# Score blocks of the prompt's attention on a third PSUM bank, the sample's results in the ring of the maxima, and a new pace for the sample beside the attention

## The chip, the cores and the metric

The kernel runs on one core of a Trainium2 chip. The metric is the device time of one execution in microseconds; lower is better. Three runs of the kernel before are shown below, and one further execution was profiled.

## What is computed

One inference step of a small decoder: one recurrent layer (RG-LRU), then one layer of forgetting attention, for a prompt of 2048 new tokens and for a *sample* of 8 sequences with 8 new tokens each, which look back on 4096 cached tokens in pages of 128 rows. There are 16 heads of 64. What the change touches is the attention, for the prompt and for the sample:

```python
def fox_block(q, k, v, cq, ck, q_pos, k_pos):
    s = jnp.einsum('bqhd,bkhd->bhqk', q, k).astype(jnp.float32) * (HEAD_DIM ** -0.5)
    s = s + jnp.swapaxes(cq, 1, 2)[:, :, :, None] - jnp.swapaxes(ck, 1, 2)[:, :, None, :]
    mask = k_pos[None, :] <= q_pos[:, None]
    s = jnp.where(mask[None, None], s, -jnp.inf)
    p = jax.nn.softmax(s, axis=-1)
    return jnp.einsum('bhqk,bkhd->bqhd', p.astype(v.dtype), v)
...
    past_k = cache_k[page_table].reshape(Bs, past_len, N_HEADS, HEAD_DIM)
    past_v = cache_v[page_table].reshape(Bs, past_len, N_HEADS, HEAD_DIM)
```

The prompt's attention is causal over 2048 positions. The sample reads every cached page, 16.8 MB of keys and values for each of 16 *turns* (a turn is one sequence and one half of the heads).

## The kernel before

The kernel's main line computes the recurrent layer, the projections, then the prompt's attention (`attention`, on the chip from about 1725 us to 2867 us), then the output projection (`project`). A second line of work, the sample (`decode`), is a Python generator that is advanced beside the main line: `Side.along(gen, share)` takes one step of the main generator, adds up the cost that it yields, and then advances the sample until the sample's own summed cost has reached `share` times that. This gives the order in which the program is written. From it a scheduler with a model of the engines' times lays down one fixed order for each engine: the earliest instruction in the program's order that is ready by the model goes first, so a later one may pass an earlier one that is not ready. On the chip each engine then goes through its list in that order and waits at semaphores. Two sample turns of the 16 (`FIRST`) lie beside an earlier stage, four and a half lie beside the projections, and the rest lies beside the attention.

**The prompt's attention.** A *unit* is one head and one of four groups of 512 queries; it has 4, 8, 12 or 16 *score blocks* of 128 keys by up to 512 queries, 640 blocks in all. For each block TensorE writes the transposed scores into a PSUM bank `st` with two matmuls (three on the diagonal, L1531, L1532, L1534), ScalarE takes the exponential into `p` (or `acc` for a unit's first block, L1540), and after each fourth block, two blocks later, `product` issues the matmuls with the values as one run (`ops`, L1551); then GpSimd adds each `p` to `acc` (L104), for the softmax's sums. The buffers: `st` has two banks, `p` has five (`NP`), `acc` five.

The maximum of each row is needed before its scores: `top` computes the scores a second time, coarsely, in the other orientation (`sx`, L1404), and VectorE reduces them (`mxs`, L1406, L1408). This runs some 8 to 18 blocks ahead of the scores. `sx` is a ring of three PSUM banks, which also takes the transposed maxima (`mps`), the sums (`tot`) and the broadcast reciprocals (`rp`).

**The sample.** A turn fetches 8 times 4 pages of keys and as many of values (`pages`, L1072, four 256 KB transfers each on SP's queue, into four buffers `raw`). VectorE transposes the keys (`ktr`, L1157); `scores` (L1125) multiplies with the queries, 64 matmul instructions in one run into a bank `dS`, which VectorE subtracts from the decay sums `sc`; `new_scores` (L1140) does it for the new rows. `softmax` uses small results `dm` (maxima) and `dsum` (sums); `products` (L1235) multiplies with the values into the bank `dO`, 16 instructions in one run; at the end `dres` (L1263) gathers the result. A run is made by `together`, which keeps its matmuls adjacent on TensorE.

**PSUM.** There are eight banks. The pool `psd` has two: tag "o" holds `dO` through a turn, tag "d" holds whichever of `dS`, `dm`, `dsum`, `dres` is in use, through `bank`. During the attention the pool `psa` has the other six: `ops` one, `st` two, `sx` three. After the sample has ended, the two banks of `psd` lie idle until the output projection. The sample's last step is followed by `project_ready`, which loads the weights of the output projection and splits them in eight steps.

The pace: `share = SHARE * (16 - FIRST) * TURN / (1024 / 128 * 24 * 4112 * 0.42 + 950000)` with `SHARE = 1.13` and `TURN = 22615`, one number for the projections and the attention. The attention yields `4.1 * (512 - lo) * 0.42` for each block and 213 for each tile of maxima.

Of the kernel before, what the change touches and what calls it, by code (L numbers as in the profile page):

```python
# [11 lines left out]
F32 = mybir.dt.float32  # L12
# [8 lines left out]
P = 128  # L21
# [6 lines left out]
H = 16  # L28
# [15 lines left out]
B_ORDER += [("g", c) for c in range(4)]  # L44

SHARE = 1.13
LEAD = 18
RAMP = 8
NS = 3
# [2 lines left out]
AHEAD = 8  # L52
FIRST = 2
NACC = 5
NP = 5
ADD = "G"
OG = 1
NQ = 6
# [14 lines left out]


SYNC = mybir.DependencyInfo(mybir.DependencyClass.Sync, mybir.DependencyReason.DATA)


def f(ap):
# [5 lines left out]
def tile_hawk_fox(  # L84
# [8 lines left out]
    V, A, G, T, S = nc.vector, nc.scalar, nc.gpsimd, nc.tensor, nc.sync  # L93
# [12 lines left out]
    def together(mms, after=()):  # L106

        first = mms[0]().ins
        for d in after:
            tc.add_manual_dep(first, d.ins.name, SYNC)  # L110
        with tc.high_priority(), tc.issue_after(first):
            for mm in mms[1:]:
                mm()


    xs_flat = x_sample.rearrange("b q d -> (b q) d")
# [94 lines left out]
    psum = {}  # L211
# [805 lines left out]
    TURN = 16 * QK + 33 * PV + 10 * HOP  # L1017


    known = set()  # L1020

    def decode(es, turns, nraw, nktr, ahead):
        pool = sbuf(es, "dec", "right")
# [25 lines left out]
        last, qbs = [], {}  # L1049

        def bank(name, tag="d"):
            return psum["dec"].tile([P, 512], F32, name=name, tag=tag, bufs=1)

        def spare():
# [52 lines left out]
        def keys(t, xs):  # L1107

            dl = t.dl
            b, hg, gmx = t.b, t.hg, t.gmx  # L1110

            def fetch_c():
                sc = t.sc = pool.tile([P, NPG // 4, 8, 32], F32, name="sc", tag="sc")
                S.dma_start(sc[:, :, :, :].rearrange("p x h i -> p (x h i)"),
                            c_d[hg, :, :, b].rearrange("m a x f -> (m a) (x f)").unsqueeze(1).to_broadcast([16, DS, 8 * 256]))
                t.cn = pool.tile([DS, 8, DS], F32, name="cn", tag="cn")
                S.dma_start(t.cn[:, :, :], cn_d[hg * 8:(hg + 1) * 8, b * DS:(b + 1) * DS].unsqueeze(0).to_broadcast([DS, 8, DS]))

            def scores(g, pp, kt):

                sp = bank("dS", "d" if ahead or pp == 0 else "o")

                def score(h, x, a):
                    blk = (h * 2 + x) * 32
                    return T.matmul(sp[a * 32:(a + 1) * 32, h * P:(h + 1) * P], qw[:, pp * 2 + h // 2, h % 2 * 2 + x, :],  # L1125
                                    kt[:, :, a, blk:blk + 32], start=(x == 0), stop=(x == 1))

                together([partial(score, h, x, a) for h in range(4) for x in range(2) for a in range(4)])
                sv = t.sc[:, g * 4:(g + 1) * 4, pp * 4:(pp + 1) * 4, :].rearrange("p n h i -> p h n i")
                tt(V, sv, sp[:, :].rearrange("p (h n i) -> p h n i", h=4, n=4), sv, ALU.subtract)  # L1130
                V.tensor_reduce(gmx[:, g, pp * 4:(pp + 1) * 4], sv, axis=AX.XY, op=ALU.max)

            def new_scores(raw):
                kx = (spare() if ahead else pool.tile([P, 512], F32, name="kx", tag="kx"))[:, :512]
                V.transpose(kx, raw[:, :])
                sp = bank("dS")

                def score(h, x):
                    blk = (h * 2 + x) * 32
                    return T.matmul(sp[:32, h * DS:(h + 1) * DS], qw[:, h // 2, h % 2 * 2 + x, :], kx[:, blk:blk + DS],  # L1140
                                    start=(x == 0), stop=(x == 1))

                together([partial(score, h, x) for h in range(8) for x in range(2)])
                tt(V, t.cn[:, :, :], sp[:DS, :64].rearrange("p (h j) -> p h j", h=8), t.cn[:, :, :], ALU.subtract)
                tt(V, t.cn[:, :, :], t.cn[:, :, :], maskN[:, :].unsqueeze(1).to_broadcast([DS, 8, DS]), ALU.add)
                V.tensor_reduce(gmx[:DS, 2, :], t.cn[:, :, :], axis=AX.X, op=ALU.max)

            for x in xs:
                g, n = divmod(x, 4)
                if n == 0:  # L1150
                    t.kts = [pool.tile([P, 4, 4, 256], F32, name="ktr", tag="ktr", bufs=nktr) for _ in range(2)]
                raw, _ = pages(cache_k, b, hg, x)
                if x == (3 if ahead else 0):
                    fetch_c()
                    t.rown = new_rows(ks_d, b, hg)
                for pp in range(2):
                    V.transpose(t.kts[pp][:, n], raw[:, :, pp * 256:(pp + 1) * 256])  # L1157
                    if n == 3:
                        dl.after(1 + pp, lambda g=g, pp=pp, kt=t.kts[pp]: scores(g, pp, kt))
                    if (g, n, pp) == (1, 0, 0):  # L1160
                        new_scores(t.rown)
                    dl.tick()
                    yield QK
# [59 lines left out]
        def values(t, xs):  # L1223

            dl = t.dl
            b, hg, sx, pc = t.b, t.hg, t.sx, t.pc
            if xs[0] == 0:
                t.op = bank("dO", "o")
            op = t.op

            def products(i, raw, came):

                def mm(d, a):
                    c = ((i + d) % 2 * 2 + a) * 32
                    return T.matmul(op[c:c + 32, :256], sx[:, d, i // 4, a * 4:(a + 1) * 4, :].rearrange("p h q -> p (h q)"),  # L1235
                                    raw[:, d, a * 256:(a + 1) * 256],
                                    start=(i + d < 2), stop=(i + d == NPG - 1))

                together([partial(mm, d, a) for d in range(4) for a in range(2)], came)

            def new_products(raw):
                for a in range(2):
                    T.matmul(op[a * 32:(a + 1) * 32, :256], pc[:, a * 32:(a + 1) * 32], raw[:, a * 256:(a + 1) * 256],
                             start=False, stop=True)

            for x in xs:
                raw, came = t.raws.pop(0) if t.raws else pages(cache_v, b, hg, x)
                dl.after(1, lambda i=x * 4, raw=raw, came=came: products(i, raw, came))
                if x == 5:
                    t.rown = new_rows(vs_d, b, hg)  # L1250
                yield 2 * PV
                dl.tick()
                yield 2 * PV
            if xs[-1] < 7:
                return
            dl.after(1, lambda: new_products(t.rown))
            dl.flush()
            ob = pool.tile([P, 256], F32, name="ob", tag="ob")
            A.copy(ob[:, :], op[:, :256])
            yield PV  # L1260
            sp = bank("dres")
            for pr in range(4):
                T.matmul(sp[:, pr * 16:(pr + 1) * 16], ob[:, pr % 2 * P:(pr % 2 + 1) * P], sel[:, pr * 16:(pr + 1) * 16],  # L1263
                         start=True, stop=True)
            for h2 in range(2):
                hp = slice(h2 * 64, (h2 + 1) * 64)
                pv_ = sp[hp, :64].rearrange("p (r h q) -> p r h q", r=4, h=2)
                rv = t.rb[hp, :].rearrange("p (r h q) -> p r h q", r=4, h=2)
                tt(V, oTs[hp, hg * 4:(hg + 1) * 4, b * DS:(b + 1) * DS], pv_[:, :, h2, :], rv[:, :, h2, :], ALU.mult)
# [37 lines left out]
    def attention(es):  # L1307
# [212 lines left out]
            yield 300  # L1520
        ops = acc = None
        pair = []
        for u, (h, qc) in enumerate(units):
            load_low(u + 2)
            for k in range(nks[u]):
# [1 line left out]
                qa, qb = qas[u], qbs[u % NQ]  # L1527
                lo = max(0, k - qc * 4) * P
                ks = slice(k * P, (k + 1) * P)
                ps = ps3.tile([P, 512], F32, name="st", tag="st", bufs=2)  # L1530
                T.matmul(ps[:, lo:], ka[:, ks], qa[:, lo:], start=True, stop=False)  # L1531
                T.matmul(ps[:, lo:], kb[:, ks], qb[:, lo:], start=False, stop=(k < qc * 4))  # L1532
                if k >= qc * 4:
                    T.matmul(ps[:, lo:lo + P], identB[:, :], causal[:, :], start=False, stop=True)  # L1534
# [38 lines left out]
                    load_head(h + 1)  # L1573
                yield 4.1 * (512 - lo) * 0.42 + (done[0] - before) * 213

    lent = {}

    rows = [(NSAMP, None, x1s_d[:, :], ys_flat)]
    rows += [(P, t, x1_d[t:t + P], yp_flat[t:t + P]) for t in range(SEQ - P, -1, -P)]
# [2 lines left out]
    def project_ready(es):  # L1582

        pool = sbuf(es, "projw", "right")
        proj["g"] = pool.tile([P, D], F32, name="bpostB")
        S.dma_start(proj["g"][:, :], b_post_norm.broadcast_to([P, D]))
        out = proj["out"] = Out(b_w_out[0], 0).place(pool)
        with ExitStack() as st:
            wpool["st"], wpool["ns"] = sbuf(st, "projs", "right"), 2
            out.fetch()  # L1590
            out.fetch()
            for i in range(8):
                yield 2000
                out.split(i + 1)
# [189 lines left out]
    def beside():  # L1784
        yield from decode(dec, turns[FIRST:], 4, 2, True)
        dec.close()
        yield from project_ready(last)

    side = Side(beside())
# [3 lines left out]
    wkeep.close()  # L1793
    lin.close()
    psum["att"] = banks(att, "psa", 6)
    side.along(attention(att), share)
    side.upto(1e12)
    project(last)
    att.close()
# [36 lines left out]
```

## Time and profile before

| | us |
|---|---|
| median of three runs | 3062.46 |
| the three runs | 3054.63, 3062.46, 3064.86 |
| the profiled execution's own time | 3055.27 |
| its span | 3053.6 |

The span is what the profile's rows cover; 1.7 us of the execution's own time lie around it. In the profile PE is TensorE, PEld its loading of weights, DVE VectorE, ACT ScalarE, POOL GpSimd, SP the engine whose queue issues nearly all transfers. L numbers are lines of the kernel. A row of waits reads "engine tile line <- what ended the wait: us in total, times, longest". TensorE's matmuls are pipelined, so that the rows of busy time overlap and a PE that is shown busy is not at its peak; the spacing of the starts is what tells its pace.

### The profile page before, as it was taken

How to read it: one execution, taken by the hardware profiler on the slowest of the kernel's cores; microseconds unless marked ns; L12 is line 12 of the kernel's file. 1: busy time of each engine (PE TensorE's matmuls, PEld its weight loads, DVE VectorE, ACT ScalarE, POOL GpSimd, SP SyncE). 2: the span in 40 equal slices, each digit the busy share in tenths (PEclk: the TensorE clock that was granted, in tenths of full speed). 3: DMA queues.
4: the chain of work that ended last, by engine and by line, in shares of the span. 5: the costliest groups of instructions: out<-in, count | busy, mean ns of one | idle time of the engine just before them, and what ended most of it. 6: DMA issues, size and time to landing. Idle time of an engine off the chain costs nothing.

```text
span 3053.6 us, 60463 instructions
## 1 busy us (share of the span) xinstructions
PE 2827.0 (93%) x21614; PEld 2258.5 (74%) x21614; DVE 1810.2 (59%) x4012; ACT 1269.8 (42%) x2874; POOL 1079.6 (35%) x1199
## 2 busy tenths in 40 slices
PE   6998999999999989998999799899899899999898
PEld 5997789988999978896888456565556565565687
DVE  7876465425357766765555566676767675554344
ACT  4665442222346655433333144343444345455311
POOL 1653201000016532000000366556465557587522
PEclk9999999999999999999999799899999999999999
DMA  4224546788622256999999988999999998323243
GB/s 122 81 85 133 175 125 203 240 268 263 216 83 89 83 185 194 316 320 320 330 311 315 294 274 268 299 275 308 306 298 319 322 297 258 92 65 86 84 145 111
DMA packets 492864, 653.41 MB, mean 214 GB/s; under 512 B 91099, under 2 KB 292828, under 8 KB 485285
## 3 DMA queue, kind: packets, MB, share of 16 engines
q1 hardware_dynamic: 488934, 643.87, 67.1%
q10 hardware_dynamic: 3340, 3.56, 0.5%
q8 instruction: 171, 2.80, 0.4%
q0 software_dynamic: 288, 2.10, 0.2%
q14 instruction: 131, 1.07, 0.1%
HBM read 513.82 MB, written 135.16 MB: 213 GB/s over the span
## 4 chain that ended last, share of the span: by engine, by line
PE 59%; DMA 18%; DVE 9%; ACT 5%; SPq 4%; issue 3%; POOL 2%; DVEq 0%; ACTq 0%; POOLq 0%
PE ops L1551 6%; PE y L368 4%; PE y L366 4%; PE y L367 4%; DMA raw<-in_cache_v_dram 4%; PE kv L366 4%; PE kv L367 4%; PE kv L368 4%; DMA raw<-in_cache_k_dram 4%; PE st L1531 3%; PE sx L1404 3%; PE dO L1235 3%; PE dS L1125 2%; PE st L1532 2%; PE qg L366 2%
## 5 line engine op out<-in xcount | busy, mean ns | idle before, releaser
L104 POOL TENSOR_TENSOR acc<-acc,p 128x512 f32<-128x512 f32 (+3 forms) x576 | 638.7, 1109 | 419.2 <-PE ops L1551 271.1
L1540 ACT ACTIVATE p<-st 128x512 f32<-128x512 f32 (+3 forms) x576 | 289.5, 524 | 404.9 <-PE st L1532 198.8
L1157 DVE STREAM_TRANSPOSE ktr<-raw 128x1024 f32<-128x1024 f32 x256 | 305.7, 1225 | 160.2 <-DMA raw<-in_cache_k_dram 157.8
L1406 DVE TENSOR_REDUCE mxs<-sx 128x1 f32<-128x512 f32 x384 | 253.1, 679 | 119.7 <-PE sx L1404 118.3
L367 PE MATMUL kv<-wl,xh 128*128 128x256 f32 (+3 forms) x1088 | 309.3, 287 | 11.2 <-DVE wl L411 11.0
L366 PE MATMUL kv<-wh,xh 128*128 128x256 f32 (+3 forms) x1088 | 310.8, 290 | 5.9 <-ACT wh L410 5.4
L368 PE MATMUL kv<-wh,xl 128*128 128x256 f32 (+3 forms) x1088 | 309.4, 287 | 0.0
L1531 PE MATMUL st<-qa,ka 128*128 128x512 f32 (+3 forms) x640 | 273.9, 428 | 12.2 <-ACT p L1540 11.0
L1551 PE MATMUL ops<-p,vvt 128*64 128x256 f32 (+1 forms) x2176 | 261.0, 366 | 3.4 <-ACT p L1540 2.8
L1404 PE MATMUL sx<-kbt,qbt 96*128 96x512 f32 (+3 forms) x640 | 236.9, 425 | 26.1 <-DMA qbt<-qd 12.0
L1532 PE MATMUL st<-qbt,kbt 128*128 128x512 f32 (+3 forms) x640 | 239.3, 374 | 0.0
L410 ACT ACTIVATE wh<-wst,gv 128x256 fp32r<-128x256 f32 (+1 forms) x384 | 164.5, 499 | 179.9 <-DMA wst<-in_b_w_in_dram 62.1
L411 DVE SCALAR_TENSOR_TENSOR wl<-wst,gv,wh 128x256 fp32r<-128x256 f32 (+1 forms) x384 | 170.5, 493 | 105.5 <-ACT wh L410 104.0
L1551 PEld LDWEIGHTS ops<-p,vvt 128*64 128x64 f32 x2176 | 161.2, 140 | 92.6 <-issue 22.7
L366 PE MATMUL qg<-xh,wh 128*128 128x384 f32 (+2 forms) x640 | 228.9, 359 | 0.0
L368 PE MATMUL qg<-xh,wl 128*128 128x384 f32 (+2 forms) x640 | 227.4, 356 | 0.0
L367 PE MATMUL qg<-xl,wh 128*128 128x512 f32 (+2 forms) x640 | 226.9, 356 | 0.0
L367 PEld LDWEIGHTS kv<-wl,xh 128*128 128x128 f32 (+1 forms) x1088 | 204.3, 189 | 14.9 <-DVE wl L411 12.6
L366 PEld LDWEIGHTS kv<-wh,xh 128*128 128x128 f32 (+1 forms) x1088 | 204.2, 189 | 12.0 <-ACT wh L410 6.4
L1090 POOL TENSOR_TENSOR qw<-qb,amask 128x128 f32<-128x128 f32 x64 | 29.3, 464 | 509.9 <-PE dS L1125 266.4
L368 PEld LDWEIGHTS kv<-wh,xl 128*128 128x128 f32 (+1 forms) x1088 | 205.6, 189 | 4.1 <-issue 4.1
L1531 PEld LDWEIGHTS st<-qa,ka 128*128 128x128 f32 x640 | 124.0, 194 | 109.9 <-issue 53.0
(297 smaller groups left out, 6370.0 us busy)
## 6 DMA issues: line engine op xcount, KB each, us to landing
raw<-in_cache_k_dram SPq DMA_DIRECT2D x512, 256.0 KB
raw<-in_cache_v_dram SPq DMA_DIRECT2D x512, 256.0 KB
wst<-in_w_kv_dram SPq DMA_DIRECT2D x48, 512.0 KB
wst<-in_b_w_in_dram SPq DMA_DIRECT2D x48, 512.0 KB
xt<-in_x_prompt_dram SPq DMA_DIRECT2D x32, 512.0 KB
wst<-in_a_w_in_dram SPq DMA_DIRECT2D x64, 256.0 KB
out_dram<-kf SPq DMA_DIRECT2D x128, 128.0 KB
sc<-cd SPq DMA_DIRECT2D x16, 1024.0 KB
```

What stands on the lines that cost most here:

```text
L104: eng.tensor_tensor(out, a, b, op=op)
L366: T.matmul(ps, lh(k), rh(k), start=(k == 0), stop=False)
L367: T.matmul(ps, lh(k), rl(k), start=False, stop=False)
L368: T.matmul(ps, ll(k), rh(k), start=False, stop=(k == nk - 1))
L411: V.scalar_tensor_tensor(wl[:, k, :], st[:, k, :], gk, f(wh[:, k, :]), op0=ALU.mult, op1=ALU.subtract)
L1157: V.transpose(t.kts[pp][:, n], raw[:, :, pp * 256:(pp + 1) * 256])
L1404: T.matmul(ps[:, :w], qb[0:96, j * P:(j + 1) * P], kb[0:96, ck * 512:ck * 512 + w], start=True, stop=True)
L1406: V.reduce_max(mx[:, j, ck:ck + 1], ps[:, :w], axis=AX.X)
L1531: T.matmul(ps[:, lo:], ka[:, ks], qa[:, lo:], start=True, stop=False)
L1532: T.matmul(ps[:, lo:], kb[:, ks], qb[:, lo:], start=False, stop=(k < qc * 4))
L1540: pair.append((k, lo, p, A.activation(p[:, lo:], ps[:, lo:], AF.Exp)))
L1551: return T.matmul(ops[r * HD:(r + 1) * HD, a0 * P:], vvs[h % 2][:, k, :], p[:, :].rearrange("p (a r c) -> p a r c", a=2, r=2)[:, a0:, r, : ...
```

## The change

Five edits:

1. `scores_bank` gives a score block its bank. As long as the sample runs, every third block takes tag "d" of `psd` and the others the two `st` banks. After the sample has ended (`dec_done`), every other block takes a bank of `psd`, "d" and "o" in turn, so that four banks go round.
2. In `decode`, once the attention's pool exists, `bank` gives what had tag "d" (`dS`, `dm`, `dsum`, `dres`) a bank of the ring `sx`, three banks shared with the maxima.
3. `together` returns its last matmul; `decode` notes it for each run of `scores` and `products`, and the first matmul of each score block gets an edge of order (no semaphore) to the last run that the program has written before it: on TensorE it is placed behind that run.
4. The sample's pace during the attention is worked out when the attention starts: what is left of the sample is spread over 88% (`SPAN`) of the attention's cost. The projections keep the former share.
5. `p` has six buffers in place of five.

```diff
+SPAN = 0.88
...
-NP = 5
+NP = 6
...
+ORDER = mybir.DependencyInfo(mybir.DependencyClass.NoSync, mybir.DependencyReason.DATA)
...
             for mm in mms[1:]:
-                mm()
+                last = mm().ins
+        return last
...
-    known = set()
+    known, run = set(), []
...
         def bank(name, tag="d"):
+            if tag == "d" and "att" in psum:
+                return psum["att"].tile([P, 512], F32, name=name, tag="sx", bufs=3)
             return psum["dec"].tile([P, 512], F32, name=name, tag=tag, bufs=1)
...
-                together([partial(score, h, x, a) for h in range(4) for x in range(2) for a in range(4)])
+                run.append(together([partial(score, h, x, a) for h in range(4) for x in range(2) for a in range(4)]))
...
-                together([partial(mm, d, a) for d in range(4) for a in range(2)], came)
+                run.append(together([partial(mm, d, a) for d in range(4) for a in range(2)], came))
...
+        wide = [0]
+
+        def scores_bank():
+
+            if dec_done:
+                wide[0] += 1
+                if wide[0] % 2:
+                    return psum["dec"].tile([P, 512], F32, name="st", tag="do"[wide[0] // 2 % 2], bufs=1)
+            else:
+                wide[0] += 1
+                if wide[0] % 3 == 0:
+                    return psum["dec"].tile([P, 512], F32, name="st", tag="d", bufs=1)
+            return ps3.tile([P, 512], F32, name="st", tag="st", bufs=2)
...
-                ps = ps3.tile([P, 512], F32, name="st", tag="st", bufs=2)
-                T.matmul(ps[:, lo:], ka[:, ks], qa[:, lo:], start=True, stop=False)
+                ps = scores_bank()
+                first = T.matmul(ps[:, lo:], ka[:, ks], qa[:, lo:], start=True, stop=False)
+                if run:
+                    tc.add_manual_dep(first.ins, run[-1].name, ORDER)
...
-    lent = {}
+    lent, dec_done = {}, []
...
         dec.close()
+        dec_done.append(True)
         yield from project_ready(last)
...
-    side.along(attention(att), share)
+    cost = sum(4.1 * 0.42 * (512 - max(0, k - qc * 4) * P) + 213 for qc in range(4) for k in range(4 * qc + 4)) * H
+    side.along(attention(att), ((16 - FIRST) * TURN - side.spent) / (cost * SPAN))
```

## The prediction

> **What bounds the kernel now.** I read the page first, then the busy time by stages, then the waits of TensorE in the two parts of the attention, then its order of instructions.
>
> ```profile
> span 3053.6 us, 60463 instructions
> PE 2827.0 (93%) x21614; PEld 2258.5 (74%) x21614; DVE 1810.2 (59%) x4012; ACT 1269.8 (42%) x2874; POOL 1079.6 (35%) x1199
> DMA  4224546788622256999999988999999998323243
> ```
>
> TensorE is the busiest throughout, and the transfers are at nine tenths or more from the middle to the 34th slice. The change touches only the attention, so I split that into the part beside the sample and the part after it. The next rows are stretches: exponentials of score blocks (busy us of ScalarE, count, granted clock, DMA share, GB/s), then the sample's key matmuls `dS` on TensorE, then the whole of one stretch.
>
> ```profile
> 1725.00:2560.00 835.00, 222.31 (x435) 0.95 0.95 297
> 1750.00:2050.00 300.00, 83.63 (x163) 0.96 0.90 275
> 2050.00:2550.00 500.00, 128.78 (x253) 0.95 0.98 308
> 2560.00:2867.00 307.00, 104.14 (x205) 0.98 0.34 94
> ...
> 1725.00:2560.00 835.00, 75.29 (x2432) 0.95 0.95 297
> 1750.00:2050.00 300.00, 23.43 (x768) 0.96 0.90 275
> 2050.00:2550.00 500.00, 47.98 (x1536) 0.95 0.98 308
> ...
> 2600.00:2850.00 250.00, 236.28 (x1345) 143.82 (x1341) 115.32 (x267) 124.67 (x282) 187.96 (x169) 0.99 0.28 77
> ```
>
> A turn has 4 runs of 64 key matmuls, 256, so part A (to 2560 us) holds 9.5 turns and 435 of the 640 blocks (68%); part B holds 205 blocks and no sample. Two stretches of A give two equations, a for a block and b for a turn: 300 = 163a + 3b and 500 = 253a + 6b. So a = 1.37 us and b = 25.6 us, and 640a + 9.5b = 877 + 243 = 1120 us of the 1142 in A and B. The same a fits a stretch with DMA at 0.90 and one at 0.98: transfers are not what paces a block. And a turn costs the same wherever it lies, so moving turns about earns nothing by itself; a or b must fall.
>
> TensorE's order shows what a contains, and why an idle column undercounts a loss:
>
> ```profile
> 2700.45 0.39 PE L1532 MATMUL st<-qbt,kbt 128*128 128x512 f32 x1
> 2700.68 0.39 PE L1404 MATMUL sx<-kbt,qbt 96*128 96x512 f32 x1
> 2701.00 0.50 PE L1531 MATMUL st<-qa,ka 128*128 128x512 f32 x1
> ...
> 2710.03 1.95 PE L1551 MATMUL ops<-p,vvt 128*64 128x256 f32 x16
> 2711.91 0.50 PE L1531 MATMUL st<-qa,ka 128*128 128x512 f32 x1
> ...
> 2700.45 0.19 PEld L1404 LDWEIGHTS sx<-kbt,qbt 96*128 96x128 f32 x1
> 2700.99 0.19 PEld L1531 LDWEIGHTS st<-qa,ka 128*128 128x128 f32 x1 [0.35 <-ACT p L1540]
> ```
>
> Starts are 0.23 us apart without a wait, and a run of 16 value matmuls for four blocks takes 1.88. A full block therefore needs 3 x 0.23 + 0.47 = 1.16 us, less on the diagonal, against a = 1.37. Where the load waited 0.35 us for ScalarE, the starts were 0.32 apart in place of 0.23: 0.09 lost. So of a wait of PEld about 0.26 us is no loss (0.35 - 0.09); the rest is.
>
> **The change part by part.** No instruction is added or taken away. The waits that the edits reach, first A, then B, then ScalarE's waits for GpSimd in A and in B:
>
> ```profile
> PEld st L1531 <- ACT p L1540: 22.4, 51, 0.8
> PEld sx L1404 <- DVE mxs L1406: 16.5, 27, 2.4
> PEld ops L1551 <- ACT p L1540: 12.9, 32, 1.0
> PEld sx L1404 <- DVE mxs L1408: 3.5, 9, 0.6
> PE dO L1235 <- DMA raw<-in_cache_v_dram: 18.7, 14, 3.3
> PE dS L1140 <- DVE sc L104: 4.3, 3, 2.3
> PE dO L1235 <- DMA raw<-in_cache_k_dram: 3.3, 2, 1.7
> PE dO L1235 <- DMA sx<-pd: 3.2, 3, 1.3
> ...
> PEld st L1531 <- ACT p L1540: 21.2, 42, 1.7
> PEld ops L1551 <- ACT p L1540: 9.7, 22, 1.5
> ...
> ACT p L1540 <- POOL acc L104: 19.3, 16, 2.8
> ACT p L1540 <- POOL acc L104: 9.8, 8, 2.5
> ```
>
> *Third (later fourth) bank for the scores.* TensorE's waits for a free `st` bank: A 22.4 - 51 x 0.26 = 9.1 us, B 21.2 - 42 x 0.26 = 10.3, together 19. A third bank lets TensorE go one block further ahead of ScalarE; I take three quarters, **-15**. Ends: 0, when ScalarE is behind by more than that block, and -44, the whole of both rows.
>
> *Sixth `p`, and the matmuls with the values.* Their waits for exponentials lose 12.9 + 9.7 - 54 x 0.26 = 8.6 us. ScalarE itself waited 29 us (19.3 + 9.8) for a `p` that GpSimd still added; a sixth buffer lets some of these exponentials go earlier. Half, **-4**; ends 0 and -23.
>
> *The sample's results in the ring.* With one bank the new rows' `dS` had to wait for VectorE to take the last run's: **-4** (the row of L1140), end 0. In return the ring of three gets more users. For a turn's time in A (435 / 9.5 = 46 blocks, as many tiles of maxima) the code puts some 55 tiles into it, and the sample adds 8: four `dS`, one of the new rows, `dm`, `dsum`, `dres`. How long each holds a bank:
>
> ```profile
> 2308.65 0.39 PE L1404 MATMUL sx<-kbt,qbt 96*128 96x512 f32 x1
> 2308.97 1.96 PE L1125 MATMUL dS<-ktr,qw 128*32 128x128 f32 x64
> ...
> 2309.08 0.70 DVE L1408 CUSTOM_DVE_ANT_0 sx<-sx,maskb 128x512 f32<-128x512 f32 x1 [0.53 <-PE sx L1404]
> 2310.99 0.69 DVE L104 TENSOR_TENSOR sc<-dS,sc 128x512 f32<-128x512 f32 x1 [0.96 <-PE dS L1125]
> ```
>
> A tile of maxima holds it 1.1 us (2308.65 to 2309.78), a `dS` 2.7 (2308.97 to 2311.68). The ring's load rises from 55 x 1.1 = 61 bank-us a turn by 8 x 2.7 = 22, a third. Waiting for VectorE at `sx` loses 16.5 + 3.5 - 36 x 0.26 = 10.6 us now; waits rise faster than the load, so I take **+6**. Ends 0 and +21, three times the present loss.
>
> *Pace.* By the code the remaining sample ends at 88% of the attention's cost, block 563 in place of 435. The pages of a turn (16.8 MB) are then asked for over 563a + 9.5b = 1014 us, not 835: 157 GB/s in place of 191, while B shows what the attention takes itself, 94. Transfers sink from a share of 0.95 to about 0.85. The waits of value runs for pages and for `sx<-pd` are 18.7 + 3.3 + 3.2 = 25 us; I take a fifth off, **-5**. Ends -20 and +25: SP's queue is in order, and the pages still stand behind the attention's own loads there, of which the worst waits 20 us for a free `qa`:
>
> ```profile
> SPq L1392 <- PE st L1534: 103.9, 12, 20.4
> ```
>
> `place_q` and its queue on GpSimd move with the turns and cost the same. The eight steps that split the output weights now lie behind block 563, where 77 blocks x 1.37 = 105 us are left; before they ran from the first load to the last split in 44 us (2558.4 to 2602):
>
> ```profile
> L465 SPq DMA_DIRECT2D wst<-in_b_w_out_dram x8: 368/392/533, 2558.4 to 2593.7; - x8
> L104 DVE TENSOR_TENSOR wol<-wst,woh x8: 1210/1309/1980, 2569.2 to 2600.8; 128x1024 fp32r<-128x1024 f32 x8
> ```
>
> They fit: **0**. Without that cover the output projection starts later, at most by some 40 us if the sample ends with the attention; I keep +15.
>
> *The order edge.* It issues nothing. Score blocks that by the model's times would have slipped ahead of a run now stand behind it, with `ops` and maxima free to pass. Taken at **0** where pages are in time; else it is the rival below.
>
> *Clock.* The granted clock is 0.95 over A and 0.99 in the stretch of B, so about 0.05 x 835 = 42 us of A's time is clock not granted. I take **0**, ends -20 and +25. The Trainium skill (TensorE: Matmul & The Clock Gate, What's actually happening) has the clock at one half after an idle window of about 3.4 us until TensorE has been busy for such a window; A's granted 0.95 beside waits of up to 3.3 us for pages agrees with that. By this rule a smoother order would earn up to those 42 us more, while its section on psum-queue depth-cycling warns that rotating through banks with small gaps can itself make the clock swing.
>
> Sum: -15 - 4 - 4 + 6 - 5 = **-22 us**. Against the profiled execution's own 3055.27 that is 3033; that execution lies 7 us under the median of 3062.46, so for the median I forecast 3062 - 22 = **3040 us**.
>
> **The rivals.**
>
> *Denser order (faster).* The fixed order is laid down with the rings in mind; with more banks and buffers it may come nearer to 1.16 us for a block, beyond the waits that I counted. For it: a is 0.2 above that. Against it: GpSimd was busy 187.96 us of 250 in B, where 172 blocks went by (1.09 us for each), so a can't go below about 1.1. If a falls by 0.10, 64 us go: 2998.
>
> *Score blocks behind late pages (slower).* TensorE is in order. A value run whose pages have not landed now holds the next score block, and with it ScalarE and GpSimd, where before a block could stand ahead. There are 12 runs a turn, 114 in all. An additional wait of 0.19 us for each is 22 us and eats the gain; that is where it decides. At 0.4 us, with half as much again of ungranted clock (+21), it costs 67 - 22 = 45 net: 3107. For it: 14 waits for value pages already, 3.3 us the longest, and SP's 20 us blocks. Against it: the lower demand, 157 GB/s.
>
> *Ring (slower).* The maxima's waits treble and drag `mps` and the row maxima with them: +21 and as much again, in place of +6: 3062 - 22 + 36 = 3076.
>
> *No change.* The counted waits give way to waits for GpSimd or to the next `ops`, and the ring eats the rest: 3062, within 9 us.
>
> **How the numbers follow.** A difference of 0.3%, 9 us, is about what a measurement of this kernel can tell from none. Forecast 0.42 (3020 to 3053, all faster), denser order 0.16, no change 0.14, late pages 0.18, ring 0.10. Faster: 0.42 + 0.16 = 0.58; same 0.14; slower 0.18 + 0.10 = 0.28. The range runs from 2990, which leaves out the lower half of the denser order, to 3095, which leaves out most of the late pages' case: some 0.2 outside.
>
> **What the profile after would show.** The waits of `st` for ScalarE fall from 43.6 us to about 15. Those of `sx` for VectorE rise from 20 to about 30. The last value run lies at 85 to 90% of the blocks, at about 2700 us, and DMA is near 0.85 until then. ScalarE's waits for GpSimd fall under 20 us. a solved anew is about 1.33, b about 25. I am wrong if the value runs' waits for pages pass 50 us or the granted clock in A falls under 0.93 (late pages), if `sx` waits 60 us (ring), if a is below 1.3 (denser), or if the sample still ends near 68% of the blocks, which would mean that the pace doesn't do what it says.

## The result, and the profile after

The changed kernel takes 3183.33 us against 3062.45: slower by 4.0%, ratio 1.0404 (95% interval 1.038 to 1.0427). The profiled execution has a span of 3180.0 us, 126 more than before. The page, and then two stretches (all engines' busy us, granted clock, DMA share, GB/s), part A up to the sample's end and part B after it; the last two rows are the exponentials of the score blocks in the same stretches:

```profile
span 3180.0 us, 60438 instructions
PE 2862.2 (90%) x21614; PEld 2281.0 (72%) x21614; DVE 1809.3 (57%) x4012; ACT 1262.3 (40%) x2874; POOL 1080.2 (34%) x1199
DMA  3225447698422468999999777778776977763243
...
1725.00:2838.00 1113.00, 947.84 (x8282) 597.36 (x8281) 632.36 (x1312) 415.12 (x1055) 571.75 (x549) 0.90 0.76 233
2838.00:2978.00 140.00, 130.81 (x773) 83.09 (x773) 70.64 (x144) 81.37 (x176) 113.55 (x98) 0.95 0.35 103
...
1725.00:2838.00 1113.00, 268.08 (x536) 0.90 0.76 233
2838.00:2978.00 140.00, 52.05 (x103) 0.95 0.35 103
```

The work is the same: TensorE has its 21614 matmuls as before. It is busy with them for 35 us longer (2827.0 us before); VectorE, ScalarE and GpSimd are within 8 us of before. The rest of the loss is waiting, and it lies in part A. Part A of the kernel before, up to its sample's end:

```profile
1725.00:2560.00 835.00, 770.72 (x7514) 489.32 (x7516) 560.31 (x1147) 350.24 (x889) 463.65 (x453) 0.95 0.95 297
```

TensorE stood for 835 - 771 = 64 us in it; now it stands for 1113 - 948 = 165. The sample now ends at 536 blocks (84%; the new pace sets 88%), and transfers have sunk to 0.76. At the prediction's prices 536 blocks and 9.5 turns need 536 x 1.37 + 9.5 x 25.6 = 977 us; part A took 1113. Part B cost what the prices say (103 x 1.37 = 141 us, 140 measured). The granted clock in A is 0.90, 0.95 before. Behind the attention's last score block 203 us follow, 187 before, but with 841 matmuls in place of 749.

TensorE's waits in the attention up to 2850 us (rows with PE), ScalarE's (rows with ACT), and TensorE's load of weights (rows with PEld): for a score block up to 2838 us and after it, then for a tile of maxima up to 2838 us:

```profile
PE dO L1240 <- DMA raw<-in_cache_v_dram: 56.6, 20, 11.6
PE dO L1240 <- DMA r<-rs: 24.3, 2, 13.1
PE mps L1426 <- DVE mrow L1422: 23.8, 16, 3.9
PE sx L1409 <- DVE mxs L1411: 12.7, 24, 3.6
...
ACT p L1561 <- PE st L1553: 252.0, 103, 32.3
ACT p L1561 <- PE st L1555: 206.8, 81, 33.8
ACT p L1561 <- POOL acc L106: 7.3, 8, 2.1
...
PEld st L1550 <- ACT p L1561: 9.6, 22, 0.8
PEld st L1550 <- ACT p L1561: 2.5, 4, 1.2
...
PEld sx L1409 <- DVE mxs L1411: 38.2, 65, 3.8
PEld sx L1409 <- DVE mxs L1413: 16.4, 34, 1.2
```

The two gains that the prediction counted are there: `st` waits 12 us for ScalarE (43.6 before), and ScalarE 7 us for GpSimd beside the sample (19.3 before). But now ScalarE waits for scores, up to 34 us at a time. From the starts of the first matmul of each block I counted the stretches of over 7 us in which no score block begins while the sample runs: 30, together 435 us; before there were 5, together 65. One of them, TensorE's order and then SP's:

```profile
2232.29 1.47 PE L1572 MATMUL ops<-p,vvt 128*64 128x256 f32 x12
2236.76 0.47 PE L1426 MATMUL mps<-ident,mrow 128*128 128x128 f32 x1 [3.00 <-DVE mrow L1422]
2237.02 0.53 PE L1208 MATMUL dsum<-ddg,ones 128*128 128x64 f32 x2
2250.65 1.93 PE L1240 MATMUL dO<-raw,sx 128*32 128x256 f32 x16 [13.11 <-DMA r<-rs]
...
2226.54 3.03 SPq L1220 DMA_DIRECT2D pd<-sy  x4
2242.08 0.43 SPq L1221 DMA_DIRECT2D sx<-pd  x1
```

A turn's first value run needs the sample's probabilities, which go out to memory (`pd`) and come back (`sx`), 24 us from the first issue to the run. TensorE stands for 13 us with the run at the head of its order. The next score block begins only at 2269.36 us, behind a second value run, a wait of 6 us for `rp` and a run of key matmuls. The row names `r<-rs`, which the run doesn't read; of what it reads, `sx` was issued last, so I take the wait to be for that, which the row doesn't show.

### The profile page after: what moved, and what is told of

The parts are those of the page before. It is cut to its first block, busy times and chain, and to the rows that moved or that the text cites. A ratio compares the mean times of both kernels' runs of the same rounds, so it can differ in the third digit from the quotient of the medians.

```text
span 3180.0 us, 60438 instructions
## 1 busy us (share of the span) xinstructions
PE 2862.2 (90%) x21614; PEld 2281.0 (72%) x21614; DVE 1809.3 (57%) x4012; ACT 1262.3 (40%) x2874; POOL 1080.2 (34%) x1199
## 4 chain that ended last, share of the span: by engine, by line
PE 48%; DMA 17%; DVE 7%; SPq 5%; ACT 3%; issue 3%; POOL 2%; DVEq 0%; ACTq 0%; POOLq 0%
PE ops L1572 6%; DMA raw<-in_cache_v_dram 4%; PE st L1550 3%; SPq L1077 3%; PE dS L1130 3%; PE dO L1240 3%; PE kv L369 3%; PE kv L370 3%; PE kv L371 3%; DMA raw<-in_cache_k_dram 3%; PE y L370 3%; PE y L369 3%; PE y L371 3%; PE st L1553 3%; PE sx L1409 2%
## 5 line engine op out<-in xcount | busy, mean ns | idle before, releaser
L1240 PE MATMUL dO<-raw,sx 128*32 128x256 f32 x2048 | 154.7, 426 | 106.8 <-DMA raw<-in_cache_v_dram 67.2
L1409 PEld LDWEIGHTS sx<-kbt,qbt 96*128 96x128 f32 x640 | 121.9, 205 | 126.5 <-DVE mxs L1411 42.9
```

What stands on the lines that cost most here:

```text
L1409: T.matmul(ps[:, :w], qb[0:96, j * P:(j + 1) * P], kb[0:96, ck * 512:ck * 512 + w], start=True, stop=True)
```

## The experiments

Eighteen kernels, in five groups; the kernels of a group are compared with the same runs of the kernel before. "After" below is the changed kernel, "end" the number of score blocks begun when the sample's last value run ended (640: it outlasted the attention).

| kernel | ring | third bank | edge | pace | p | us | ratio to before (95%) | end |
|---|---|---|---|---|---|---|---|---|
| before | | | | former | 5 | 3062 | | 435 |
| after | all | yes | yes | 88% | 6 | 3183 | 1.0404 (1.038, 1.0427) | 537 |
| a1_no_edge | all | yes | | 88% | 6 | 3150 | 1.0287 (1.0259, 1.0315) | 545 |
| a2_old_pace | all | yes | yes | former | 6 | 3239 | 1.0595 (1.0562, 1.0627) | 640 |
| b1_edge | | | yes | former | 5 | 3057 | 0.9996 (0.9972, 1.0021) | 435 |
| b2_banks | all | yes | | former | 5 | 3202 | 1.0468 (1.0434, 1.0501) | 640 |
| b3_pace | | | | 88% | 5 | 3070 | 1.0027 (1.001, 1.0044) | 435 |
| c1_ring | all | | | former | 5 | 3179 | 1.0391 (1.0361, 1.0421) | 640 |
| c2_st3_sx2 | | from the ring | | former | 5 | 3180 | 1.038 (1.0349, 1.0411) | 378 |
| c3_four_late | | after the sample (never taken) | | former | 5 | 3059 | 0.9997 (0.998, 1.0014) | 435 |
| d1_ring_pace | all | | | 88% | 5 | 3137 | 1.0269 (1.0236, 1.0303) | 549 |
| d2_no_bank | all | | yes | 88% | 6 | 3202 | 1.0479 (1.0443, 1.0515) | 533 |
| d3_small_ring | small | | | former | 5 | 3103 | 1.0163 (1.0126, 1.02) | 640 |
| d4_ring4 | all, 4 banks | | | former | 5 | 3144 | 1.0282 (1.0246, 1.0318) | 640 |
| f1_small_pace | small | | | 88% | 5 | 3071 | 1.0039 (1.0017, 1.006) | 547 |
| f2_dS_pace | dS | | | 88% | 5 | 3116 | 1.019 (1.0168, 1.0211) | 549 |
| f3_small_span97 | small | | | 97% | 5 | 3057 | 0.9988 (0.9972, 1.0003) | 593 |
| f4_small_late_np6 | small | after the sample | | 94% | 6 | 3032 | 0.9916 (0.9896, 0.9937) | 578 |
| g1_np6 | | | | former | 6 | 3053 | 0.9975 (0.9964, 0.9987) | 434 |
| g2_small_np6 | small | | | 94% | 6 | 3049 | 0.9959 (0.9944, 0.9975) | 577 |

**First group: which part.** The profile after had made the edge the suspect.

a1_no_edge, from after:

```diff
-                if run:
-                    tc.add_manual_dep(first.ins, run[-1].name, ORDER)
```

> The changed kernel (3183 us) without the order edge from a score block to the sample's last run; third bank, ring, pace and sixth p stay. Theory E (the edge holds score blocks behind value runs that wait for the sample's probabilities and pages): the 30 stretches of over 7 us without a score block, 435 us in all, fall to the 5 and 65 us of before, the granted clock beside the sample comes back from 0.90 to about 0.95, and the time is 3040 us, between 3015 and 3065. Theory P (the pace alone, by which the sample lasts to 86% of the blocks, costs it): still above 3150. Theory R (the sample's results hold the banks of the maxima): still above 3130, with the waits of sx for VectorE unchanged.

a2_old_pace, from after:

```diff
-    side.along(attention(att), ((16 - FIRST) * TURN - side.spent) / (cost * SPAN))
+    side.along(attention(att), share)
```

> The changed kernel with the former share for the attention in place of the new pace; edge, third bank, ring and sixth p stay. Theory E in its first form (the edge holds blocks at any pace): 3120 us or more. Theory E in its second form (the edge binds only because the new pace writes the runs into the program before their data can be there; with the former share the runs are written later than they are ready): 3030 to 3070. Theory P: 3030 to 3070 as well, with the sample's end back near 68% of the blocks. Theory R: above 3130.

b1_edge is before with the two lines that a1 takes out (and `run` filled as in the change):

> The kernel before (3062 us) with the order edge alone; former banks, ring, pace and five p. Theory E, first form: 3120 or more. Theory E, second form: the edge seldom binds at the former share, 3062 within 20. Theories P and R: 3062 within 9.

b2_banks is before with `scores_bank` and the change's `bank`:

> The kernel before with the third bank for the scores (four after the sample) and the sample's results in the ring of the maxima; no edge, former pace, five p. Theory E and theory P: a gain as the prediction counted for the banks, 3035 to 3060, with the waits of st for ScalarE down from 43.6 us to about 15. Theory R: slower than 3080, with the waits of sx for VectorE at 60 us or more.

The suspect fell. The edge alone costs nothing (0.9996); taken out of the change it gives back 33 of the 121 us. Without it 21 of the stretches with no score block remain, together 320 us, and the clock beside the sample is still 0.90; the theory had 5 stretches and 0.95. The former pace makes the change slower still. The banks alone, third bank and ring together, cost more than the whole change, and there the sample outlasts the attention.

**Second group: ring, third bank or pace.** c1_ring is before with these lines; c2_st3_sx2 is before with `bufs=3` at each `st` and `bufs=2` at each `sx`; c3_four_late keeps of `scores_bank` only the part under `dec_done`; b3_pace is before with the change's last two lines.

```diff
         def bank(name, tag="d"):
+            if tag == "d" and "att" in psum:
+                return psum["att"].tile([P, 512], F32, name=name, tag="sx", bufs=3)
```

> The kernel before with one part alone: during the attention the sample's dS, dm, dsum and dres take banks of the maxima's ring of three; tag d lies idle, the scores keep two banks, former pace, five p, no edge. Theory S (starvation: the sample's runs go into openings that the attention leaves because it has only two score banks; a third bank closes them and the sample falls back to its place in the program, so that it outlasts the attention): 3062 within 15, sample's end near 68% of the blocks. Theory R (the ring shared with the sample holds maxima and sums back, and score blocks with them): 3110 or more, with ten or more stretches of over 7 us without a score block, 5 before.

> The kernel before with the third score bank taken from the maxima's ring, which keeps two; the sample keeps its own bank d, former pace, five p, no edge. Theory S: the sample outlasts the attention (all 640 blocks issued before its last value run) and the time is 3130 or more. Theory R alone: the sample ends near 68% as before, and the time is 3040 to 3090, whatever two maxima banks cost.

> The kernel before with the score blocks going round four banks only after the sample has ended (d and o of the sample's pool beside the two st); nothing changed while the sample runs. Both theories: no loss, 3035 to 3060; the sample's end stays at 435 blocks, and of the 21.2 us that st waits for ScalarE after it at least half goes.

> The kernel before with the new pace alone (what is left of the sample spread over 88% of the attention's cost); former banks, five p, no edge. Theory S: the sample's place in the program matters little while it goes into openings: it ends between 60 and 75% of the blocks and the time is 3062 within 20. Theory P (spreading costs in itself): 3090 or more, the sample's end near 86%.

Theory S fell on both sides. With a third score bank from elsewhere the sample ends *earlier* (378 blocks), and the ring by itself makes it outlast the attention. Theory R had c2 at 3090 us at most, and missed it too. In c2 the attention's last block starts at 2994.0 us, 2866.4 before, and TensorE's waits for the maxima are longer (up to 2560 us `sx` for the first `mxs` row 13.3 us, 7.2 before; `mps` 13.3, 6.2 before). So I read it that three maxima banks are not plenty, and that the ring was the attention's tight resource, which the change opened to the sample; c2 also gives the scores a bank, and no run parts the two.

c3 tests nothing. By the code the former share writes about four turns of 14 beside the projections and 640 x 962 x 0.279 / 22615 = 7.6 beside the attention (0.279 is the share, 962 the mean cost of a block, 22615 that of a turn). The sample thus ends behind the attention in the program, `dec_done` is set too late, and no score block takes a late bank (nor does one in a2 and b2, at the same pace). After the sample `st` waits 21.0 us for ScalarE, as before (21.2).

The rows of c1_ring: value runs and score blocks (min/median/max ns, first and last start), then the exponentials in two stretches and the key matmuls in the first:

```profile
L1240 PE MATMUL dO<-raw,sx x2048: 376/379/637, 643.4 to 2949.5; 128*32 128x256 f32 x187
L1550 PE MATMUL st<-qa,ka x640: 222/411/796, 1723.8 to 2792.5; 128*128 128x512 f32 x160
...
1725.00:2793.00 1068.00, 327.71 (x639) 0.95 0.70 212
2793.00:2950.00 157.00, 0.28 (x1) 0.64 0.87 281
...
1725.00:2793.00 1068.00, 58.64 (x1920) 0.95 0.70 212
```

The attention is done 74 us earlier than before; then the sample runs alone for 157 us, and the output weights, which are split behind it, delay the projection: from the last start of the two to the span's end it is 3176.6 - 2949.5 = 227 us, before 3053.6 - 2866.4 = 187.

Why does the sample lag? The key matmuls in stretches of before, c1_ring, d3_small_ring (below) and b3_pace:

```profile
1750.00:2550.00 800.00, 71.40 (x2304) 0.96 0.95 296
1750.00:2750.00 1000.00, 56.71 (x1856) 0.95 0.69 209
1750.00:2750.00 1000.00, 65.82 (x1982) 0.98 0.75 228
1750.00:2550.00 800.00, 74.29 (x2304) 0.96 0.93 289
```

By the code a turn stands 22615 / 0.279 / 962 = 84 blocks apart at the former pace. Before, 2304 / 256 = 9.0 turns went by beside 416 blocks, 46 for each: the sample ran far ahead of its place. In c1_ring 7.25 turns went by beside about 600 blocks (640 in 1068 us): 83 for each. The sample goes at its place in the program. And b3_pace, with its own bank, goes ahead as before although the program has it earlier. That tiles of one ring are handed out in the program's order is my inference from these counts; I call it the tie.

**Third group: the tie, or too few banks.** d1_ring_pace is c1_ring with the change's pace, d2_no_bank is after with `st` in its two banks, d3_small_ring has in `bank` the condition `and name != "dS"`, d4_ring4 is c1_ring with every fourth tile of maxima in tag d:

```diff
+            rung[0] += 1
+            if rung[0] % 4 == 0:
+                ps = psum["dec"].tile([P, 512], F32, name="sx", tag="d", bufs=1)
+            else:
+                ps = ps3.tile([P, 512], F32, name="sx", tag="sx", bufs=3)
```

> The kernel before with the ring for the sample's results and the new pace; scores in two banks, five p, no edge. Theory O (order: the tiles of one ring are handed out in the program's order, so the sample can no longer run ahead of its place in the program, and maxima written behind a sample's tile wait for it): the sample ends where the program has it, 84 to 88% of the blocks, no longer behind the attention as at the former pace (3179 us), and the time is 3100 to 3160, with score blocks held back for over 150 us. Theory L (load: three banks are too few for both): as slow as the ring alone, 3160 or more.

> The changed kernel (3183 us) with the scores back in two banks; ring, edge, pace and sixth p stay. This prices the third bank inside the change. As the prediction counted it (15 us gain): 3190 to 3210. Theories O and L, in which the pace of the score blocks is set by the ring and the third bank finds nothing to earn: 3183 within 20.

> The kernel before with only dm, dsum and dres in the ring (three short tiles a turn, none of the dS); dS keeps bank d, former pace, two score banks, five p, no edge. Theory O: three tiles a turn are enough to tie the sample to its place, it outlasts the attention and the time is 3130 or more. Theory L: little load, 3062 to 3090, the sample's end below 75% of the blocks.

> The ring alone (3179 us) with a fourth bank: every fourth tile of maxima takes the idle tag d, the sample's results and the rest stay in the ring of three. Theory O: no help, the sample still outlasts the attention, 3150 or more. Theory L: 3120 or less.

Three small tiles a turn suffice to tie the sample: 1982 / 256 = 7.7 turns beside about 625 blocks (640 in 1024 us), 81 for each, and it outlasts the attention, with four maxima banks too. The times were less bad than I had said for this theory, 3103 and 3144 in place of 3130 and 3150 at least: in d3 the attention itself was done at 2751.6 us. So I read it that both hold: the tie says where the sample ends, the load adds to what it costs. The stretches of over 7 us without a score block fit that: 9, together 82 us, in c1 (I had ten or more), and 3, together 25 us, in d3; d1 has 17, together 193. d2 prices both banks of `scores_bank` inside the change, the third beside the sample and the four after it: 3202 without them, 3183 with them, 19 us earned (23 by the two ratios to before).

**Fourth group: what costs at the new pace.** f1_small_pace is d3_small_ring with the pace, f2_dS_pace has `and name == "dS"` in its place, f3_small_span97 is f1 with `SPAN = 0.97`, f4_small_late_np6 is f1 with `SPAN = 0.94`, `NP = 6` and the late banks of c3.

> dm, dsum and dres in the ring, dS in bank d, new pace (88%); two score banks, five p, no edge. Theory D (the four dS of a turn, held from their first matmul until VectorE has subtracted them, crowd the maxima out): 3010 to 3060, the sample's end at 84 to 88% of the blocks, fewer than 8 stretches of over 7 us without a score block. Theory T (the tie alone: whatever of the sample stands in the ring makes the maxima behind it wait for late pages): 3100 to 3150, with over 150 us in such stretches.

> Only dS in the ring, the three small results in bank d, new pace; two score banks, five p, no edge. Theory D: 3110 to 3150, like the whole ring at this pace (3137). Theory T: the same. Were the small results the cause: 3060 or less.

> As f1, with the sample spread over 97% of the attention's cost. With the small ring at the former pace the attention alone ended after 1024 us and the sample outlasted it by 119; the 1.6 turns that were left would cost 41 beside it. Theory D: 3015 to 3060, within 20 of f1. Theory T: 3090 or more.

> As f1, spread over 94%, with the sixth p and, after the sample has ended, four score banks. Theory D: 10 us under f1 at most, 3005 to 3055. Theory T: 3090 or more.

At one pace and one place of the sample (547 to 549 blocks), the whole ring costs 80 us (d1), only `dS` 56 (f2), only the small results 11 (f1). Theory D holds in the main: it is the `dS` of a turn, four and the one of the new rows. f1 lies 11 us over what I gave it, with 11 stretches, together 95 us, where I had fewer than 8. The pace alone had cost 9 us (b3, 1.0027, its interval overlaps f1's), so this doesn't show that something is left of the tie. TensorE's waits up to 2780 us, f1 first, then f2:

```profile
PE dO L1240 <- DMA raw<-in_cache_v_dram: 21.6, 17, 3.5
PE mps L1426 <- DVE mrow L1422: 8.2, 5, 3.2
...
PE dO L1240 <- DMA raw<-in_cache_v_dram: 20.1, 13, 4.9
PE mps L1426 <- DVE mrow L1422: 18.6, 10, 5.9
PE sx L1409 <- DVE sc L106: 7.4, 5, 2.9
```

The value runs wait alike. With `dS` in the ring a tile of maxima waits for VectorE's subtraction (`sc`), and the row maxima come late (`mrow`). That fits the crowding, though these rows hold only 18 us of the 45 between the two; the rest stays open, and I did not take the fixed order apart.

f3 brought the time to that of before, and f4 is faster than both kernels: 3032 us, 0.9916, a gain of under 1%.

**Fifth group: what earns in f4.** g1_np6 is before with `NP = 6`; g2_small_np6 is f4 without the late banks.

> The kernel before with six p in place of five, nothing else. If the sixth p earns what ScalarE waits for GpSimd (19.3 us beside the sample, 9.8 after it): 3030 to 3050. As the prediction counted it: 3056. If it only helps a sample that is tied to its place: 3060 within 8.

> As f4 without the four late banks: small results in the ring, 94%, six p, two score banks throughout. If the sixth p makes f4's gain: 3030 to 3045. If the four late banks do: 3055 to 3065, as f1 and f3.

The sixth `p` earns 0.25% by itself (8 us; the prediction had 4). f4 is below g2 by 17 us, with a 0.9916 whose interval doesn't touch 0.9959's: there the late banks pay (13 us by the two ratios). g2 itself came between the two ranges that I had set for it. The gain lies after the sample: f4 did its last 62 blocks in 85 us, g2 its last 63 in 116, and 203 us followed the last block in f4, 187 in g2. c3 could not show this, as no block took a late bank in it. f4's stretches, up to the sample's end and after:

```profile
1725.00:2737.00 1012.00, 940.60 (x8589) 601.39 (x8588) 656.14 (x1374) 452.93 (x1130) 608.29 (x585) 0.97 0.85 261
2737.00:2823.00 86.00, 78.19 (x466) 50.04 (x465) 45.45 (x81) 49.54 (x101) 77.64 (x60) 0.96 0.37 115
```

## Why the prediction was wrong

*The step that failed is the sample's results in the ring.* The prediction priced this edit as load: 22 bank-us a turn on 61, +6 us, at most +21. By itself this edit costs 118 us (c1_ring against its own runs of before). Two things were missing. First, a ring shared by two streams of work ties them: my text called the freedom of the sample to pass an unready block a feature of the order, but I did not see that the sample's *own bank* gave it that freedom (46 blocks to a turn before, 83 in c1; that the ring does it is inferred from these counts). Second, the load was not mild: at one and the same place of the sample the `dS` cost 69 us (80 in d1, 11 in f1, each against its own runs of before). The waits of `sx` for VectorE that I scaled up (20 us) show little of it: they are 25 us beside the attention in c1_ring. In the changed kernel they are 55, where I had 30 and named 60 as the sign of this rival. It may be that the fixed order is laid around the full ring beforehand; no run shows that. The rival "ring" had the right part and about a third of the size: it put +42 us in place of +6. No run takes the ring alone out of the change, as the third score bank is the one that it frees. But the whole can be built up, by the ratios to before: ring and pace cost 82 us (d1), the edge and the sixth `p` another 64 (d2), and the score banks take back 23 (after).

*The score banks* came near their size, in part by luck. Counted were 15 us, about half of them beside the sample. The waits went as counted (`st` for ScalarE 12 us, 40 in d2 with its two banks), and inside the change both banks together earn 19 to 23 us. But when the sample ends, the changed kernel has begun 537 blocks and d2 533 at the same time (2839 us): beside the sample the third bank earned some 4 x 1.37 = 5 us, and most came from the four banks after it. Without the edge the third bank did not pay: b2 is 23 us slower than c1, whose only difference is that bank, and a1 is no faster than d1 (1.0287, 1.0269), though it has all the banks and the sixth `p`. Why, I did not find out. The sixth `p` was right (4 counted, 8 measured).

*The pace* was put at -5 for the transfers. Alone it is 1.0027, and it does not even move the sample (435 blocks), because an untied sample takes its own place. My sentence that turns earn nothing by being moved holds for the pace alone, but not under the tie: f3 is 14 us faster than f1, and only the sample's place differs (593 blocks, 547). The sign that the sample still ends near 68% came true for the pace alone; inside the change the ring makes the sample obey it. There the pace is a repair: 3239 without it (a2), 3183 with it.

*The order edge* was put at 0, and alone that is so. On top of the other four edits it costs 33 us (3150 without it, 3183 with it), and with two score banks 65 (d1 against d2, though d2 also has the sixth `p`). Its mechanism is close to the rival "late pages": TensorE stands at a turn's first value run, though in the stretch above for its probabilities more likely than for pages. From the trace, the gaps of TensorE before the ten first runs are 43 us with it, 4 without it, 8 before. The signs that I had set for that rival came true (page waits over 50 us, clock 0.90), but they misled: a1, without the edge, has page waits of 50.0 us and a clock of 0.90 as well. That rival gave 3107 and an edge to blame, and the larger part needed no edge. Signs that several causes share don't tell them apart.

*The output weights* were given a cover, with some 40 us if it went. It held in the changed kernel, where the last split begins at 2880.7 us and the last score block at 2977.3. It went in c1_ring, where the tail after the last value run grew by 40 us (227 against 187), with 840 matmuls in it in place of 749.

*The equations for a and b* fit some kernels and not others. c1_ring's 639 blocks and 7.5 turns (1920 / 256) should take 639 x 1.37 + 7.5 x 25.6 = 1067 us and took 1068. d3_small_ring's key matmuls while its attention runs:

```profile
1725.00:2752.00 1027.00, 70.07 (x2112) 0.98 0.75 231
```

That is 2112 / 256 = 8.25 turns beside 639 blocks; by the prices 1087 us, measured 1027. In the changed kernel part A is 136 us over them. So a and b are no fixed prices, and the prediction's reading that transfers don't pace a block rests on two stretches of one kernel. Its reading of the page's DMA row was a little generous, too: three of the slices that it calls nine tenths or more show 8.

## What to carry to other kernels

A buffer that one stream of work has to itself is also its freedom to run ahead or fall back; putting two streams into one ring made one pace of two here, and three small tiles a turn were enough for it. Price a shared ring by who must now wait for whom in the written order, not only by bank time, and find out first which ring is scarce (here moving one bank from the maxima to the scores cost as much as the whole change). Where a change has five parts, each part alone and the whole less each part are worth more than the waits of the whole: here the longest waits named the edge, which was the smaller cause. And make sure that the edit that a run is to test takes effect in it: c3 gave "no gain" for banks that no block took.

## What the runs showed of the hardware

The clock follows the waits more than I had allowed. The granted clock was 0.95 beside the sample before, 0.90 in the changed kernel, 0.97 in f4, and 0.64 in c1_ring's stretch of the sample alone, where TensorE is busy for less than half of the time (72 us of 155). The Trainium skill (TensorE: Matmul & The Clock Gate, What's actually happening) has the array fall to half rate after an idle window of about 3.4 us; waits of 11 to 13 us for a value run and a clock between a half and one agree with that. But the traces show more drops than such waits. Their record of the clock knows only 1.0 and 0.5, and a stretch at 0.5 lasts 3.4 us or a multiple of it (but for the last of a run); 27 of these begin in part A of the changed kernel and 10 in part A before, while TensorE stood for longer than 3.4 us in one piece only ten times and once. So most drops came without so long a wait, and the waits of up to 3.3 us that the prediction named don't account for its 0.95 by that rule.

Part A of the changed kernel lacks 0.10 x 1113 = 111 us of clock, 42 before. What this cost is less, since the clock is also low while TensorE waits: its busy time for the same 21614 matmuls grew by 35 us, an estimate of the slower clock's price, beside some 100 us more of standing in part A.
